# Edges of issue order among the small products of an RWKV-7 and attention block

## The chip, the cores and the metric

The kernel runs on one core of one Trainium2 chip. The metric is device time in microseconds of that core. Before the change the median of three runs is 1573.8 us (1572.52 to 1575.09).

## The reference, cut to what matters

One decoder layer over 1024 tokens of width 1024. An input projection feeds two branches: sliding-window attention, and an RWKV-7 recurrence whose decay and rate come from two low-rank ("lora") products. Both are merged, projected, and followed by a squared-ReLU MLP. The change touches the recurrence alone:

```python
w_log = -softplus(-(decay_bias + tanh(token_shift(w_p, mu_w)) @ decay_up)) - 0.5
decay = exp(-exp(w_log))
a = sigmoid(aaa_bias + token_shift(a_p, mu_a) @ aaa_up)
...
def step(S, inp):                                   # per head, per token
    sa = einsum('bhij,bhj->bhi', S, a_t)
    S = S * w_t + sa[..., None] * b_t + v_t[..., None] * k_t
    return S, einsum('bhij,bhj->bhi', S, r_t)       # y_t
```

The kernel does not step token by token. It cuts the 1024 tokens into 16 chunks of 64, solves each chunk's triangular system by small matrix products, and carries the state from chunk to chunk.

## The kernel before, in words

The program is written in Python with tile pools; a scheduler orders each engine's instructions by priority and by when it reckons that their inputs are ready, and that fixed order is what the chip runs. TensorE (PE) therefore issues in an order chosen at build time.

Up to about 658 us the kernel does projections, attention and the recurrence together. The recurrence is eight *units*: four pairs of heads times two halves of the sequence. Each unit has three steps:

- `unit_e` (L458 on): two lora products with three passes each into two PSUM tiles `ps_l` (L472 to L474); decays, keys and rates from them on ScalarE and VectorE; then chunk scores `ps_s`, two groups (`par` 0 and 1) of eight products, four for each head of the pair, into two PSUM tiles (L519 to L524). Head 0 lies on partitions 0 to 63 and head 1 on 64 to 127, so each product uses 64 rows of the array. Both `ps_l` and `ps_s` come from the PSUM pool tag "s", which has two buffers. VectorE masks the scores into `SA` and `SR`, and solves the 16-wide diagonal blocks row by row in `LT` (L565, L566).
- `unit_m` (L570 on): the 16-wide inverses come back through DRAM as `XT`, are transposed into `XD`, and are widened to 64 by small products `ps_z` and `ps_x`; `ps_g` holds 16 products of the masked scores with the values.
- `unit_c` (L622 on): the *chain* over eight chunks. Per chunk: `ry` (state times keys and receptances), a VectorE add into `G`, two products `pu` (64x64), a VectorE copy into `UV`, product `pd`, two VectorE updates of the state `sbd`, and the next `ry`. Behind it 16 products `py` (128 rows, 64 columns of the array) give the output of the unit (L660 to L665). A `py` needs only the `UV` of its own chunk.

The steps of a unit have high priority. What stands between them on TensorE is filled with low-priority work: projections `ps_m` (128x128 weights, 512 columns), the attention products `ps_t`, `pt_t` and `po`, and transposes `pt`. Nothing in the source binds the products of one `ps_l`, `ps_s` or `py` group to each other: the scheduler is free to take them in any order that their inputs allow.

Of the kernel before, what the change touches and what calls it, by code (L numbers as in the profile page):

```python
# [2 lines left out]

# [55 lines left out]
def hybrid_block(ctx, tc, x_ap, xt_ap, win_ap, lora_ap, wbr_ap, wout_ap, wff1_ap, wff2_ap, cst_ap,  # L59
                 vec_ap, eye_ap, amk_ap, out_ap, dbg=None):  # L60
    nc = tc.nc
    V, A, G, PE = nc.vector, nc.scalar, nc.gpsimd, nc.tensor
# [93 lines left out]
    def mm3(out, pairs):  # L156
        n, last = 0, 3 * len(pairs) - 1
        for (lh, ll), (rh, rl) in pairs:
            for a, b in ((ll, rh), (lh, rl), (lh, rh)):
                PE.matmul(out=out, lhsT=a, rhs=b, start=(n == 0), stop=(n == last))  # L160
                n += 1

    def proj(w, xh, xl, hf, nk=NK):
        ps = pm.tile([P, HALF], F32, tag="m", name="ps_m")
        sl = slice(hf * HALF, (hf + 1) * HALF)
        mm3(ps, [(w[k], (xh[k][:, sl], xl[k][:, sl])) for k in range(nk)])
        return ps
# [71 lines left out]
    def phase1():  # L239
# [27 lines left out]
        g0, g1, full = slice(0, 64), slice(64, 128), slice(0, 128)  # L267
# [190 lines left out]
        def unit_e(p, hf, lw, X):  # L458
            lwh, lwl = lw
            la = ep.tile([P, 2, HALF], F32R, tag="la", name="la")  # L460
# [4 lines left out]
            UV = rp.tile([P, 8, 128], F32, tag="UV", name="UV", bufs=2)  # L465
            BKt = rp.tile([P, 8, 128], F32, tag="BKt", name="BKt", bufs=2)
            SA = rp.tile([P, 2, 8, 64], F32, tag="SA", name="SA", bufs=2)
            SR = rp.tile([P, 2, 8, 64], F32, tag="SR", name="SR", bufs=2)
            bv = rp.tile([P, HALF], F32, tag="bv", name="bv", bufs=2)
            wc = rp.tile([P, 8], F32, tag="wc", name="wc", bufs=2)  # L470
            lps = [pp.tile([P, HALF], F32, tag="s", name="ps_l") for _ in range(2)]
            for n, (a, b) in enumerate(((lwl, 0), (lwh, 1), (lwh, 0))):  # L472
                for ps, rows in zip(lps, (g0, g1)):
                    PE.matmul(out=ps, lhsT=a[rows], rhs=la[rows, b], start=(n == 0), stop=(n == 2))  # L474
            tha = ep.tile([P, HALF], F32, tag="tha", name="tha", bufs=1)
            A.activation(out=tha, in_=lps[1], func=AF.Tanh, scale=0.5, bias=hb[:, 4 + p:5 + p])
            ps = lps[0]
# [39 lines left out]
            ARf = AR.rearrange("p a (b s) c -> p a b (s c)", s=2)  # L517
            BKf = BK.rearrange("p a (b s) c -> p a b (s c)", s=2)
            for par in range(2):  # L519
                pss = [pp.tile([P, 4, 2, 64], F32, tag="s", name="ps_s") for _ in range(2)]  # L520
                for i in range(4):
                    for h in range(2):
                        PE.matmul(out=pss[h][:, i], lhsT=BKf[h * 64:h * 64 + 64, i, par],  # L523
                                  rhs=ARf[h * 64:h * 64 + 64, i, par], start=True, stop=True)  # L524
                for h in range(2):
                    for i, dst in enumerate((SA, SR)):
                        slot = (par + i) % 2
                        V.tensor_mul(out=dst[:, par, h::2, :], in0=pss[h][:, :, slot, :],
                                     in1=mk[:, i].unsqueeze(1).broadcast_to([P, 4, 64]))
# [32 lines left out]
            for t in range(1, 16):  # L562
                n = min(t, 8)
# [58 lines left out]
        def unit_c(p, hf, X):  # L622
            us = slice(hf * HALF, (hf + 1) * HALF)
            ARf, UV, BKt, SR, bv, wc, G0, XT = (X[n] for n in ("ARf", "UV", "BKt", "SR", "bv", "wc", "G0", "XT"))
            Yt = rp.tile([P, 4, 2, 64], F32, tag="Yt", name="Yt", bufs=2)
            for c in range(8):
                par, cp = c % 2, c // 2
                first = hf == 0 and c == 0
                uc, vc = slice(64 * par, 64 * par + 64), slice(64 - 64 * par, 128 - 64 * par)
                cur, nxt = sbd[par], sbd[1 - par]  # L630
                ry = pp.tile([P, 2, 64], F32, tag="r", name="ry", bufs=1)
                Rs = G0[:, cp, :]
                if first:
                    G.memset(Yt[vc, cp], 0.0)
                else:
                    PE.matmul(out=ry.rearrange("p a b -> p (a b)"), lhsT=ARf[:, cp, par], rhs=cur, start=True,  # L636
                              stop=True)
                    V.tensor_add(out=Rs[uc], in0=Rs[uc], in1=ry[uc].rearrange("p a b -> p (a b)"))
                    A.copy(out=Yt[vc, cp], in_=ry[vc])
                pu = pp.tile([P, 128], F32, tag="c", name="pu", bufs=1)  # L640
                for h in range(2):
                    PE.matmul(out=pu[uc, h * 64:h * 64 + 64], lhsT=XT[uc, 2 * cp + h],  # L642
                              rhs=Rs[uc, h * 64:h * 64 + 64], start=True, stop=True)
                V.tensor_copy(out=UV[uc, c, :], in_=pu[uc])
                if hf == 0 or c < 7:
                    pd = pp.tile([P, 128], F32, tag="c", name="pd", bufs=1)
                    PE.matmul(out=pd, lhsT=BKt[:, c], rhs=UV[:, c], start=True, stop=True)  # L647
                    if not first:
                        sw = rp.tile([P, 128], F32, tag="sw", name="sw", bufs=2)
                        A.activation(out=sw, in_=cur, func=AF.Copy, scale=wc[:, c:c + 1])  # L650
                    for h in range(2):
                        hs = slice(h * 64, h * 64 + 64)
                        if first:
                            V.tensor_scalar(out=nxt[hs, hs], in0=pd[hs, hs], scalar1=wc[hs, c:c + 1],
                                            scalar2=None, op0=ALU.mult)
                        else:
                            V.scalar_tensor_tensor(out=nxt[hs, hs], in0=pd[hs, hs], scalar=wc[hs, c:c + 1],
                                                   in1=sw[hs, hs], op0=ALU.mult, op1=ALU.add)
            py = pp.tile([P, 4, 2, 64], F32, tag="y", name="py", bufs=1)
            for cp in range(4):  # L660
                for h in range(2):
                    for par in range(2):
                        vc = slice(64 - 64 * par, 128 - 64 * par)
                        PE.matmul(out=py[vc, cp, h], lhsT=SR[:, par, 2 * cp + h, :],  # L664
                                  rhs=UV[:, 2 * cp + par, h * 64:h * 64 + 64], start=True, stop=True)  # L665
            V.tensor_add(out=Yt, in0=Yt, in1=py)
            if hf == 0:
                dump(f"Yt{p}", Yt)

            Yv = Yt.rearrange("p a b c -> p (a b) c")  # L670
            mean = rp.tile([P, 8], F32, tag="mean", name="mean", bufs=1)
            V.tensor_reduce(out=mean, in_=Yv, axis=AX.X, op=ALU.add)
            V.tensor_scalar(out=mean, in0=mean, scalar1=1.0 / 64, scalar2=None, op0=ALU.mult)
            V.tensor_sub(out=Yv, in0=Yv, in1=mean.unsqueeze(2).broadcast_to([P, 8, 64]))
            ysq = rp.tile([P, 8, 64], F32, tag="ysq", name="ysq", bufs=1)
            A.activation(out=ysq, in_=Yv, func=AF.Square)
            var = rp.tile([P, 8], F32, tag="var", name="var", bufs=1)
            V.tensor_reduce(out=var, in_=ysq, axis=AX.X, op=ALU.add)
            rs = newton(ep, var, 8, 1.0 / 64, GN_EPS, tag="y")
            V.tensor_mul(out=Yv, in0=Yv, in1=rs.unsqueeze(2).broadcast_to([P, 8, 64]))  # L680
            y = rp.tile([P, HALF], F32, tag="ysq", name="y", bufs=1)
            pt = pp.tile([P, 4, 2, 64], F32, tag="y", name="pt", bufs=1)
            for i in range(4):
                PE.transpose(pt[:, i], Yt[:, i], ident)
            for par in range(2):
                A.activation(out=e4(y)[:, :, par, :], in_=pt[:, :, 1 - par, :], func=AF.Identity,
                             scale=v_("lng", p), bias=v_("lnb", p))
            V.tensor_add(out=y, in0=y, in1=bv)
            nc.sync.dma_start(out=yr_d[p][:, us], in_=y)
# [86 lines left out]
    for ct in range(NK):  # L776
        wa = load_w(wbr_ap[ct][:, 0:4], 4)
        wb = load_w(wbr_ap[ct][:, 4:8], 4)
        for hf in range(2):
# [5 lines left out]
            ps = proj(wa, yh, yl, hf, 4)  # L785
            V.scalar_tensor_tensor(out=ga, in0=ga, scalar=1.0, in1=ps, op0=ALU.add, op1=ALU.mult)
            ps = proj(wb, yh[4:], yl[4:], hf, 4)
# [9 lines left out]
    h = [fpool.tile([P, T], F32, name=f"h{k}") for k in range(NK)]  # L797
# [114 lines left out]
    pss = [(pm if t == "m" else pp).tile([P, HALF], F32, tag=t, name="ps_o", bufs=n) for t, n in tags]  # L912
# [43 lines left out]
    for i in range(16):  # L956
# [4 lines left out]
        ps = prod(split_w(a11), "B11")  # L961
# [4 lines left out]
        ps = prod(split_w(s1), "T1")  # L966
# [4 lines left out]
        ps = prod(split_w(s2), "T2")  # L971
# [8 lines left out]
        ps = prod(split_w(s3), "T3")  # L980
# [12 lines left out]
        ps = prod(w4, "B22")  # L993
        V.tensor_add(out=u2, in0=u2, in1=ps)
        c12 = relu_sq("c12", u2, u2, 1)
        ps = prod(split_w(a12), "B21")
        V.tensor_add(out=p1, in0=p1, in1=ps)
        c11 = relu_sq("c11", p1, p1, 0)
        ps = prod(split_w(a22), "T4")
# [3 lines left out]
        for q in range(2):  # L1003
            w = load_w(wff2_ap[i, 2 * q], 4) + load_w(wff2_ap[i, 2 * q + 1], 4)
            for hf in (1, 0):
                sl = slice(hf * HALF, (hf + 1) * HALF)
                for c in range(4):
# [3 lines left out]
                    ps = pp.tile([P, HALF], F32, tag=tag, name="ps_f", bufs=2 if tag == "s" else 1)  # L1011
# [99 lines left out]
```

## Time and profile before

| | us |
|---|---|
| median of three runs | 1573.8 |
| profiled execution, whole time | 1569.57 |
| its span, first to last instruction | 1567.8 |
| TensorE busy | 1538.9 (98%) |
| VectorE busy | 1053.5 (67%) |
| ScalarE busy | 612.2 (39%) |

Busy time is the time in which at least one instruction of the engine is under way. Matmuls overlap, so what one costs is better read in the timeline as the time from its start to the start of what follows it. In that timeline a float32 product appears as two passes (a group of eight scores is "x16"), a float32r product and a transpose as one. The profiled execution is 4.2 us shorter than the median of the runs.

### The profile page before, as it was taken

The page shows a single profiled execution, that of the slowest core. Times are in us where ns is not written, and L with a number is a line of the kernel's source. Part 1 is how long each engine was busy: PE and PEld are TensorE (multiplying, and loading weights), DVE is VectorE, ACT ScalarE, POOL GpSimd, SP SyncE. Part 2 cuts the span into 40 slices and gives each one's busy share as a digit, 9 for nine tenths or more (in the row PEclk, how much of TensorE's full clock was granted, in tenths as well). Part 3 has the DMA queues.
Part 4 walks back from the last instruction along what each step waited for, and adds up shares of the span by engine and source line. Part 5 has one row for each costly group of instructions (what it writes and reads, how often), then busy time and mean ns, then how long its engine had stood idle before and what let it go on. Part 6 is the DMA issues. An engine that isn't in the chain of part 4 may idle for free.

```text
span 1567.8 us, 23163 instructions
## 1 busy us (share of the span) xinstructions
PE 1538.9 (98%) x8588; PEld 1232.9 (79%) x8588; DVE 1053.5 (67%) x2420; ACT 612.2 (39%) x1238; POOL 14.3 (1%) x54
## 2 busy tenths in 40 slices
PE   5999999999999999999999999999999999999999
PEld 5878777777777777788888778888888888888887
DVE  5233877888898775344557587777777777777776
ACT  7333345465545556432224433332333222222222
POOL 1000000000000000000000000000000000000000
PEclk9999999999999999999999999999999999999999
DMA  5465243333221323383442021111111111111113
GB/s 186 155 178 144 95 123 120 103 109 104 82 88 60 97 89 123 109 293 121 143 162 85 20 68 54 43 52 54 54 54 55 43 52 47 54 48 47 47 41 114
DMA packets 108993, 145.72 MB, mean 93 GB/s; under 512 B 27472, under 2 KB 49872, under 8 KB 108880
## 3 DMA queue, kind: packets, MB, share of 16 engines
q1 hardware_dynamic: 108880, 144.23, 28.5%
q8 instruction: 68, 1.11, 0.3%
q14 instruction: 45, 0.37, 0.1%
HBM read 108.54 MB, written 35.65 MB: 92 GB/s over the span
## 4 chain that ended last, share of the span: by engine, by line
PE 93%; DVE 4%; DMA 1%; ACT 1%; issue 0%; SPq 0%; DVEq 0%; ACTq 0%
PE ps_m L160 34%; PE ps_f L160 22%; PE ps_p L160 19%; PE po L160 2%; PE pu L642 2%; PE ps_o L917 1%; PE ps_s L523 1%; PE py L664 1%; PE pk L236 1%; PE pt_t L378 1%; PE ry L636 1%; PE pd L647 1%; PE ps_l L474 1%; PE ps_t L341 1%; PE ps_z L595 1%; PE pt L219 1%
## 5 line engine op out<-in xcount | busy, mean ns | idle before, releaser
L160 PE MATMUL ps_m<-ul,whi 128*128 128x512 f32 x576 | 233.8, 406 | 0.0
L160 PE MATMUL ps_m<-uh,wlo 128*128 128x512 f32 x576 | 233.2, 405 | 0.0
L160 PE MATMUL ps_m<-uh,whi 128*128 128x512 f32 x576 | 232.9, 404 | 0.0
L1013 DVE TENSOR_TENSOR h<-h,ps_f 128x512 f32<-128x512 f32 x256 | 174.5, 687 | 86.3 <-PE ps_f L160 79.8
L145 DVE TENSOR_TENSOR wlo<-wraw,whi 128x512 fp32r<-128x512 f32 x165 | 113.6, 688 | 75.8 <-ACT whi L144 73.6
L144 ACT CAST whi<-wraw 128x512 fp32r<-128x512 f32 x169 | 104.4, 618 | 147.2 <-PE ps_m L160 70.0
L160 PE MATMUL ps_p<-T,whi 128*128 128x512 f32 x512 | 160.3, 394 | 0.0
L160 PEld LDWEIGHTS ps_m<-ul,whi 128*128 128x128 f32 x576 | 108.4, 188 | 20.8 <-issue 0.5
L160 PEld LDWEIGHTS ps_m<-uh,wlo 128*128 128x128 f32 x576 | 108.4, 188 | 20.3 <-issue 0.4
L160 PEld LDWEIGHTS ps_m<-uh,whi 128*128 128x128 f32 x576 | 108.5, 188 | 20.1 <-issue 0.6
L160 PE MATMUL ps_p<-B,whi 128*128 128x512 f32 x384 | 119.6, 392 | 0.0
L160 PEld LDWEIGHTS ps_p<-T,whi 128*128 128x128 f32 x512 | 96.9, 189 | 22.9
L144 ACT CAST whi<-wst 128x512 fp32r<-128x512 f32 x64 | 39.7, 621 | 178.0 <-PE ps_f L160 178.0
L160 PE MATMUL ps_p<-T,wlo 128*128 128x512 f32 x256 | 102.2, 399 | 1.3 <-DVE wlo L145 1.3
L160 PEld LDWEIGHTS ps_p<-B,whi 128*128 128x128 f32 x384 | 72.1, 188 | 16.9
L160 PE MATMUL ps_p<-B,wlo 128*128 128x512 f32 x192 | 76.1, 396 | 0.0
L145 DVE TENSOR_TENSOR wlo<-wst,whi 128x512 fp32r<-128x512 f32 x64 | 44.3, 692 | 39.4 <-ACT whi L144 39.4
L144 ACT CAST whi<-fraw 128x512 fp32r<-128x512 f32 x48 | 29.9, 622 | 87.6 <-PE ps_f L160 61.5
L160 PEld LDWEIGHTS ps_p<-T,wlo 128*128 128x128 f32 x256 | 48.4, 189 | 12.1 <-DVE wlo L145 1.4
L145 DVE TENSOR_TENSOR wlo<-fraw,whi 128x512 fp32r<-128x512 f32 x48 | 33.1, 692 | 31.4 <-ACT whi L144 31.2
L160 PE MATMUL ps_f<-c12h,wlo 128*128 128x512 f32 x128 | 50.4, 394 | 0.0
L160 PE MATMUL ps_f<-c22h,wlo 128*128 128x512 f32 x128 | 50.4, 394 | 0.0
(305 smaller groups left out, 3190.9 us busy)
## 6 DMA issues: line engine op xcount, KB each, us to landing
wraw<-win SPq DMA_DIRECT2D x72, 256.0 KB, 3.0
fraw<-wff SPq DMA_DIRECT2D x64, 256.0 KB, 2.8
wraw<-wff SPq DMA_DIRECT2D x64, 256.0 KB, 2.6
gate_d<-gt SPq DMA_DIRECT2D x32, 256.0 KB, 2.1
z_d<-zt SPq DMA_DIRECT2D x24, 256.0 KB, 2.3
xt<-x SPq DMA_DIRECT2D x8, 512.0 KB, 5.5
la<-wa_d SPq DMA_DIRECT2D x8, 512.0 KB, 4.6
aq<-q_d SPq DMA_DIRECT2D x8, 512.0 KB, 4.3
```

The lines of the kernel that those rows point to most:

```text
L144: A.copy(out=hi, in_=raw)
L145: (eng or V).tensor_sub(out=lo, in0=raw, in1=hi.bitcast(F32))
L160: PE.matmul(out=out, lhsT=a, rhs=b, start=(n == 0), stop=(n == last))
L219: PE.transpose(pt[:, i * 128:(i + 1) * 128], xs[i][:, k * 128:(k + 1) * 128], ident)
L236: PE.matmul(out=ps_out[:, col + 2 * i:col + 2 * i + 2], lhsT=sq[:, i * 128:(i + 1) * 128], rhs=c_("ind"), start=True, stop=True)
L341: PE.matmul(out=ps[:, i, w0:], lhsT=q_[:, g, j], rhs=k_[:, 2 + g, w0:], start=True, stop=False)
L378: PE.transpose(pt[:, sb, i], sm[:, i, sb * 128:(sb + 1) * 128], ident)
L474: PE.matmul(out=ps, lhsT=a[rows], rhs=la[rows, b], start=(n == 0), stop=(n == 2))
L523: PE.matmul(out=pss[h][:, i], lhsT=BKf[h * 64:h * 64 + 64, i, par], rhs=ARf[h * 64:h * 64 + 64, i, par], start=True, stop=True)
L595: PE.matmul(out=ps[uc, l], lhsT=SA[uc, par, l], rhs=XD[uc, l], start=True, stop=True)
L642: PE.matmul(out=pu[uc, h * 64:h * 64 + 64], lhsT=XT[uc, 2 * cp + h], rhs=Rs[uc, h * 64:h * 64 + 64], start=True, stop=True)
L1013: V.tensor_add(out=h[ct][:, sl], in0=h[ct][:, sl], in1=ps)
```

## The change

A helper `in_order` issues a list of matmuls with an edge from each to the next one: it binds their order on TensorE, adds no semaphore, and leaves other instructions free to stand between them. It is used for

- the six `ps_l` products of a unit: half a (rows 0 to 63, decay) and half b (rows 64 to 127, rate) in turn,
- the eight `ps_s` products of a group: head 0 and head 1 in turn,
- the two `pu` products of a chunk,
- the 16 `py` products of a unit, which also get an edge from the last `pu` of the chain, so that none of them stands inside the chain.

```diff
+    def in_order(mms, after=None):
+        for out, lhsT, rhs, start, stop in mms:
+            with tc.issue_after(after) if after is not None else nullcontext():
+                after = PE.matmul(out=out, lhsT=lhsT, rhs=rhs, start=start, stop=stop).ins
+        return after
...
-            for n, (a, b) in enumerate(((lwl, 0), (lwh, 1), (lwh, 0))):
-                for ps, rows in zip(lps, (g0, g1)):
-                    PE.matmul(out=ps, lhsT=a[rows], rhs=la[rows, b], start=(n == 0), stop=(n == 2))
+            in_order([(ps, a[rows], la[rows, b], n == 0, n == 2)
+                      for n, (a, b) in enumerate(((lwl, 0), (lwh, 1), (lwh, 0)))
+                      for ps, rows in zip(lps, (g0, g1))])
...
-                for i in range(4):
-                    for h in range(2):
-                        PE.matmul(out=pss[h][:, i], lhsT=BKf[h * 64:h * 64 + 64, i, par],
-                                  rhs=ARf[h * 64:h * 64 + 64, i, par], start=True, stop=True)
+                in_order([(pss[h][:, i], BKf[h * 64:h * 64 + 64, i, par], ARf[h * 64:h * 64 + 64, i, par], True, True)
+                          for i in range(4) for h in range(2)])
...
-                for h in range(2):
-                    PE.matmul(out=pu[uc, h * 64:h * 64 + 64], lhsT=XT[uc, 2 * cp + h],
-                              rhs=Rs[uc, h * 64:h * 64 + 64], start=True, stop=True)
+                last = in_order([(pu[uc, h * 64:h * 64 + 64], XT[uc, 2 * cp + h], Rs[uc, h * 64:h * 64 + 64], True,
+                                  True) for h in range(2)])
...
-            for cp in range(4):
-                for h in range(2):
-                    for par in range(2):
-                        vc = slice(64 - 64 * par, 128 - 64 * par)
-                        PE.matmul(out=py[vc, cp, h], lhsT=SR[:, par, 2 * cp + h, :],
-                                  rhs=UV[:, 2 * cp + par, h * 64:h * 64 + 64], start=True, stop=True)
+            outs = [slice(64, 128), slice(0, 64)]
+            in_order([(py[outs[par], cp, h], SR[:, par, 2 * cp + h, :],
+                       UV[:, 2 * cp + par, h * 64:h * 64 + 64], True, True)
+                      for cp in range(4) for h in range(2) for par in range(2)], last)
```

Every engine keeps the same instructions; only their order differs, on TensorE between the instructions that run at 147 and at 658 us before. In the changed kernel the bound matmuls all stand under line 166, and other lines are 3 to 6 higher.

TensorE, one chunk of the chain of the fourth unit, before: from its `pd` to the `pu` of the next chunk.

```order
L647 MATMUL pd<-UV,BKt 128x128
L664 MATMUL py<-UV,SR 64x64
L160 MATMUL ps_m<-uh_144,wlo 128x512
L160 MATMUL ps_m<-ul_152,whi 128x512
L160 MATMUL ps_m<-uh_144,whi 128x512
L160 MATMUL ps_m<-uh_145,wlo 128x512
L160 MATMUL ps_m<-ul_153,whi 128x512
L636 MATMUL ry<-sbd_489,AR 128x128
L160 MATMUL ps_m<-uh_145,whi 128x512
L160 MATMUL ps_m<-uh_146,wlo 128x512
L160 MATMUL ps_m<-ul_154,whi 128x512
L642 MATMUL pu<-G_3681,XT 64x64 x2
```

One `py`, whose `UV` has just come, stands between `pd` and the work that fills the time until `ry`.

The same engine and unit after the change: from the last `pd` of the chain on.

```order
L650 MATMUL pd<-UV,BKt 128x128
L160 MATMUL ps_m<-uh_149,wlo 128x512
L160 MATMUL ps_m<-ul_157,whi 128x512
L160 MATMUL ps_m<-uh_149,whi 128x512
L160 MATMUL ps_m<-uh_142,wlo 128x512
L160 MATMUL ps_m<-ul_150,whi 128x512
L640 MATMUL ry<-sbd_489,AR 128x128
L160 MATMUL ps_m<-uh_142,whi 128x512
L160 MATMUL ps_m<-uh_143,wlo 128x512
L160 MATMUL ps_m<-ul_151,whi 128x512
L166 MATMUL pu<-G_3681,XT 64x64 x2
L166 MATMUL py<-UV,SR 64x64 x13
```

The `py` is gone from between `pd` and `ry`, and 13 of the unit's 16 stand behind its last `pu`; one `ps_m`, the other three and the 16 `ps_g` of the next unit follow.

In the whole program before, the 128 `py` stand in 65 runs: 33 of one, 31 of three and one of two, 57 of them right behind a `pd`. After, they stand in 14 runs, all behind the last `pu` of a unit: two of 16, and six groups of 16 that are cut once. Adjacent matmuls of different tile shape become fewer by 98 (424 before, 326 after), while entries from a 128x128 product into one of 64 rows and 128 columns rise from 27 to 35.

TensorE, the second score group of the second unit, before; `ps_s_1886` is head 0, `ps_s_1887` head 1.

```order
L523 MATMUL ps_s_1886<-AR_1795,BK_1796 128x128 x4
L160 MATMUL ps_m_1765<-uh2_144,whi_1727 128x512
L523 MATMUL ps_s_1887<-AR_1795,BK_1796 128x128 x4
L160 MATMUL ps_m_1765<-uh3_145,wlo_1728 128x512
L549 MATMUL pt_1913<-cst_80,BK_1796 128x128 x4
```

The two heads run one after the other, four products each.

The same group after.

```order
L166 MATMUL ps_s_1886<-AR_1795,BK_1796 128x128
L160 MATMUL ps_m_2143<-uh0_142,whi_2133 128x512
L160 MATMUL ps_m_2143<-uh1_143,wlo_2134 128x512
L166 MATMUL ps_s_1887<-AR_1795,BK_1796 128x128
L166 MATMUL ps_s_1886<-AR_1795,BK_1796 128x128
L166 MATMUL ps_s_1887<-AR_1795,BK_1796 128x128
L166 MATMUL ps_s_1886<-AR_1795,BK_1796 128x128
L166 MATMUL ps_s_1887<-AR_1795,BK_1796 128x128
L166 MATMUL ps_s_1886<-AR_1795,BK_1796 128x128
L166 MATMUL ps_s_1887<-AR_1795,BK_1796 128x128
```

The first product still goes ahead alone, since the second PSUM buffer comes free later; the other seven now alternate. Of the 16 score groups seven alternated without a gap before and five do after. Nine groups ran in blocks of one head or in pieces before, and 11 are cut after, seven of these in the form above. Of the eight lora groups one alternates without a gap after; in seven half a's first product goes ahead alone (up to 61 other matmuls before half b's), and the other five follow alternately, in four units with one more gap.

## Rows read from the trace of the kernel before

**Rows 1.** Page, chain that ended last: share of the span by engine.
```profile
PE 93%; DVE 4%; DMA 1%; ACT 1%; issue 0%; SPq 0%; DVEq 0%; ACTq 0%
```

**Rows 2.** Windows: length, busy PE, PEld, DVE, ACT, POOL, clock, DMA; changed stretch.
```profile
147.00:658.00 511.00, 505.50 (x4018) 387.24 (x4018) 389.78 (x1357) 274.21 (x671) 6.64 (x34) 1.00 0.32 100
```

**Rows 3.** Waits of PE, 147 to 658 us: total, times, longest.
```profile
PE ps_s L523 <- DVE SR L528: 1.2, 2, 0.7
...
PE ry L636 <- DVE sbd L657: 0.2, 1, 0.2
```

**Rows 4.** Timeline of PE, one chunk: start, duration, engine, line, operation.
```profile
393.30 0.38 PE L647 MATMUL pd<-UV,BKt 128*128 128x128 f32 x2
393.62 0.33 PE L664 MATMUL py<-UV,SR 128*64 128x64 f32 x2
393.87 0.50 PE L160 MATMUL ps_m<-uh,wlo 128*128 128x512 f32 x1
394.21 0.39 PE L160 MATMUL ps_m<-ul,whi 128*128 128x512 f32 x1
...
395.14 0.38 PE L636 MATMUL ry<-sbd,AR 128*128 128x128 f32 x2
...
395.59 0.40 PE L160 MATMUL ps_m<-uh,wlo 128*128 128x512 f32 x1
```

**Rows 5.** Timeline of PE, a run of three py behind pd.
```profile
336.43 0.38 PE L647 MATMUL pd<-UV,BKt 128*128 128x128 f32 x2
336.74 0.45 PE L664 MATMUL py<-UV,SR 128*64 128x64 f32 x6
337.12 0.51 PE L160 MATMUL ps_m<-uh,wlo 128*128 128x512 f32 x1
337.46 0.40 PE L160 MATMUL ps_m<-ul,whi 128*128 128x512 f32 x1
```

**Rows 6.** Timeline of PE, 16 products ps_g in one run.
```profile
291.01 1.15 PE L579 MATMUL ps_g<-UV,SA 64*64 64x64 f32 x32
292.09 0.51 PE L160 MATMUL ps_m<-uh,wlo 128*128 128x512 f32 x1
```

**Rows 7.** Timeline of PE: scores alternating, four of one head, one alone.
```profile
409.78 1.16 PE L523 MATMUL ps_s<-AR,BK 64*128 64x128 f32 x16
410.87 0.51 PE L160 MATMUL ps_m<-uh,wlo 128*128 128x512 f32 x1
...
193.39 1.13 PE L523 MATMUL ps_s<-AR,BK 64*128 64x128 f32 x8 [0.56 <-DVE SR L528]
194.44 0.49 PE L160 MATMUL ps_m<-uh,whi 128*128 128x512 f32 x1
...
275.79 0.49 PE L523 MATMUL ps_s<-AR,BK 64*128 64x128 f32 x2
276.20 0.33 PE L664 MATMUL py<-UV,SR 128*64 128x64 f32 x2
```

**Rows 8.** Timeline of PE: lora, three of one half, then four alternating.
```profile
147.14 0.49 PE L474 MATMUL ps_l<-la,lwl 64*128 64x512 f32 x1
...
148.03 0.83 PE L236 MATMUL pk<-cst,sq 128*128 128x2 f32 x6
...
475.14 0.49 PE L474 MATMUL ps_l<-la,lwl 64*128 64x512 f32 x1
...
475.81 0.49 PE L636 MATMUL ry<-sbd,AR 128*128 128x128 f32 x2
```

**Rows 9.** Timeline of DVE, the state update in the chunk of rows 4.
```profile
393.79 0.58 DVE L657 SCALAR_TENSOR_TENSOR sbd<-pd,wc,sw 64x64 f32<-64x64 f32 x2 [0.24 <-PE pd L647]
```

**Rows 10.** Timeline of DVE, then PE: the inverse of one unit arrives.
```profile
510.25 0.71 DVE L591 STREAM_TRANSPOSE XD<-XT 128x512 f32<-128x512 f32 x1
...
511.18 1.15 PE L595 MATMUL ps_z<-XD,SA 64*64 64x64 f32 x32
```

More of the change, by code (lines that the diff above doesn't have):

```diff
@@ L1 @@
-from contextlib import ExitStack
+from contextlib import ExitStack, nullcontext
 import math
```

## The prediction

> **What bounds the kernel now.** I read the chain of waits first, then the windows, then TensorE's waits, and the timeline last. The chain that ended last is 93% TensorE and 4% VectorE [rows 1]. The change moves matmuls only between 147 and 658 us, so the question is what bounds that stretch. In its 511 us TensorE is busy 505.5 and VectorE 389.8, and the clock is at its full level, 1.00, which is 2.4 GHz [rows 2]. TensorE's waits there are small: the scores waited 1.2 us in all for a buffer, the chain once, for 0.2 us [rows 3]. So the stretch costs what the matmuls cost in the order in which they stand. No instruction is removed or added; the whole effect must come from what each costs beside its neighbours, less the waits that a tighter order opens. The reader should therefore look in the timeline at start-to-start times, and not at the durations, which overlap.
>
> **The y products.** In the chunk of rows 4 the time from `pd` to the second matmul behind its `py` is 394.21 - 393.30 = 0.91 us. A float32 product of the same shape without a `py` stands a little later: from `ry` to the second `ps_m` behind it is 395.59 - 395.14 = 0.45 us [rows 4]. One `py` thus costs 0.46 us there, of which 0.25 us lies between its own start and the next matmul's; the rest is that `pd` and the next `ps_m` run longer. A run of three costs 337.46 - 336.43 = 1.03, less the same 0.45, that is 0.58 us, and 0.38 us of it by its own start-to-start [rows 5]. The order before has 19 runs of one and 12 of three between a `pd` and a `ps_m`: 19 x 0.46 + 12 x 0.58 = 15.7 us. The other 14 of one, 19 of three and one of two stand beside other things (attention products, transposes, other small products), where part of the price is due anyway; I take their own time, 14 x 0.25 + 19 x 0.38 + 0.3 = 11.0 us. Together 26.7 us. After the change there are eight groups of 16. The nearest row is `ps_g`: 16 small products in 292.09 - 291.01 = 1.08 us [rows 6]; it has 64 rows where `py` has 128, but the same 64 columns and 64 outputs, and alternates places in the same way. That gives 8 x 1.08 = 8.6 us. Six groups are cut once; a cut is one more way out of and into the small shape, and between nothing and 0.46 us I take 0.3, so 1.8 us. Saved: 26.7 - 10.4 = 16.3 us. The lower bound has all 65 runs at their own time (20.3 us) against 10.4: 9.9 us. The upper has all at full price (33.5 us) and the cuts free: 24.9 us.
>
> In rows 4 a change of tile shape and back costs about 0.4 us beyond what a product in a run costs (1.08/16 = 0.07). The Trainium skill, TensorEngine Tiling (Array Packing), section Tiling Modes, states this as a rule: a change of mode, not just of tile, drains TensorE. By that rule the 98 changes fewer are the gain, at half of 0.4 us each some 20 us, near my sum; it also speaks against the part on scores below, where such entries rise from 27 to 35.
>
> **The chunk scores.** A group that alternates costs 410.87 - 409.78 = 1.09 us; four products of one head cost 194.44 - 193.39 = 1.05, so a group in two blocks 2.1; one product alone costs 276.20 - 275.79 = 0.41 us [rows 7]. Before: seven groups at 1.09 and nine at about 2.0 (some of the nine alternate in part): 25.6 us. After: five at 1.09; seven with one product ahead, 0.41 + 1.05 = 1.46; four in other pieces, which I put at 1.7: 5.5 + 10.2 + 6.8 = 22.5 us. Eight more entries at 0.1 to 0.2 us take back about 1. I take a gain of 2 us. Bounds: if all 16 cost 1.09, a gain of 8; if the 11 cut ones cost 2.1, a loss of 3, or 5 with the entries.
>
> **The lora products.** Three of one half cost 148.03 - 147.14 = 0.89 us, so a group in blocks 1.78; four in turn cost 475.81 - 475.14 = 0.67, so six 1.0 us [rows 8]; one alone I take from the scores, 0.41 [rows 7]. Before: four groups in blocks and four alternating in part, which I put at 1.5: 13.1 us. After: seven with one ahead and five in turn, 0.41 + 1.0, one at 1.0, and 0.2 for each of four gaps: 11.7 us. Gain 1.4 us, between 0 and 5. Half a's result, which the decays need, now comes after half b has its buffer; in the longest case 61 other matmuls stand between. I cost this at nothing, because the scores that need it stand many matmuls later; where that cover is gone it is a wait at `ps_s`. The `pu` pairs already stand together: nothing.
>
> The sum is 16.3 + 2 + 1.4 = 19.7 us of TensorE time, with 5 and 38 as the ends of all bounds together.
>
> **What comes back as waits.** Two covers become thinner. First, each chunk: `ry` needs `sbd`. In rows 4 and 9 the update ends at 393.79 + 0.58 = 394.37 and `ry` starts at 395.14, 0.77 us later. Without the `py`, 0.46 us of this goes and 0.31 is left (0.19 where three stood). There are 60 such places, and one waited before [rows 3]; behind a waiting `ry` the whole queue of TensorE stands. VectorE runs other work between, so some updates will be late by a few tenths. Between nothing and 60 x 0.2 = 12 us I take 3. Second, each unit: `XD` ends at 510.25 + 0.71 = 510.96 and `ps_z` starts at 511.18 [rows 10], so this unit's products come hardly later than their input. If the way of the inverse through VectorE and DRAM does not move, TensorE gives back there what it won in the unit, 19.7 / 8 = 2.5 us, in all eight 19.7. But VectorE is busy only 389.8 of 511 us [rows 2] and itself waits for `pd` in part [rows 9], so most of its work moves forward with TensorE; I take 2. Together 5 us come back.
>
> The `py` at the end of a unit make its output later by at most one group, 1.1 us. The norm and the store that follow are hidden by projections that fill TensorE; without them it would cost that 1.1 us at the last unit alone. No DMA is added.
>
> Net 19.7 - 5 = 14.7 us. The profiled execution took 1569.6 us (its span 1567.8 and 1.8 around it), so I expect 1554.9 of such an execution; the median of the runs is 4.2 higher, so 1573.8 - 14.7 = 1559.1 us.
>
> **The rivals.**
> - *More comes back.* The tighter order meets late inputs at most chunks and half the units: 8 + 5 = 13 us come back, 1567 us. For it: covers of 0.3 us in rows 4 and 9, and 0.2 in rows 10. Against: VectorE has 24% free.
> - *All comes back.* The period of a unit is set by the inverse and not by TensorE; then the 19.7 us turn into waits at `ps_z` and `ry`: 1574 us. Against it: TensorE waits for almost nothing now [rows 3], while a chain that set the period would already show in them.
> - *Slower: the strict turns stall the queue.* With alternation the second product of a group must wait until its own PSUM buffer is free, and TensorE issues in order, so everything behind it waits too. Before, a whole head could run in that time; now one product does, 0.41 us. There are 24 such groups; from 19.7 / 24 = 0.8 us of wait each the gain is gone, and at 1.0 us each the kernel takes 1573.8 + 24 - 19.7 = 1578 us. For it: two such waits exist, up to 0.7 us [rows 3]. Against: the order after puts two or more `ps_m` between the first product and the second in most groups.
> - *More than my sum.* Each change of tile shape costs the full half of 0.46 us wherever it stands: 98 x 0.23 = 22.5, with the 3.4 us of scores and lora 25.9, and nothing comes back: 1548 us. It is what the rule of the Trainium skill on changes of mode (TensorEngine Tiling (Array Packing), section Tiling Modes) would do here; rows 4 to 6 bear it out so far.
>
> **How the numbers follow.** My forecast has 62% (its own range 1552 to 1565), more coming back 16%, all coming back 10%, the stall 5%, more than the sum 7%. The range from 1550 to 1568 holds the first two and part of the last, and leaves out what is above. About 0.2% (3 us) is what a measurement of this kernel can tell from no change. Faster by more than that: forecast, more coming back and more than the sum, with a little taken for ends: 85%; within it 9%; slower 6%.
>
> **What the profile after would show.** Right: `py` in eight groups of about 1.1 us, its busy time by line far under the present one; TensorE busy in the changed stretch about 485 us; `pd` followed by `ps_m` at 0.45 to 0.55 us for both; waits of TensorE for `sbd`, `XD` or `SR` of some 5 us. Wrong: groups of `py` near 3 us each, or a TensorE whose idle time before `ry`, `ps_z` and `ps_s` grows by more than 10 us.

## The result and the profile after

The changed kernel takes 1558.3 us (median of four, 1557.45 to 1559.07), the kernel before in the same comparison 1574.2 us (1572.52 to 1575.09): a ratio of 0.990, with a 95% interval of 0.988 to 0.992. It is faster by 16 us; 1559.1 was forecast, in a range of 1550 to 1568. The profiled execution took 1557.75 us (span 1556.0); that is only 11.8 us under the profiled one of before, which was 4.2 us faster than the median of its kernel. What the traces account for below is therefore the 11.8, and not the whole 16.

The chain that ended last, as in [rows 1]:

```profile
PE 89%; DVE 7%; DMA 2%; ACT 1%; issue 1%; SPq 0%; DVEq 0%; ACTq 0%
```

TensorE still sets the time, but VectorE's share has grown from 4 to 7%, as it would if some inputs now came late. The windows, with the columns of [rows 2]; the changed stretch now ends near 646 us:

```profile
147.00:646.00 499.00, 490.10 (x4022) 370.47 (x4022) 386.16 (x1358) 274.60 (x673) 6.71 (x34) 1.00 0.34 105
```

The stretch is 12 us shorter at the same clock (13.2 us between the same two instructions). What lies ahead of it is the same 147 us. What lies behind it takes 910.0 us instead of 909.8, or 1.3 more from the second of those two instructions on. TensorE's idle time in it rises from 511.0 - 505.5 = 5.5 to 8.9 us. Its waits there, as in [rows 3] (total, times, longest):

```profile
PE ps_t L347 <- DMA ak<-k_d: 1.8, 2, 1.5
PE ps_s L166 <- DVE SR L532: 0.9, 2, 0.6
PE pt L553 <- DVE SR L532: 0.8, 2, 0.5
PE ps_z L615 <- DVE DZ L611: 0.7, 1, 0.7
PE ry L640 <- DVE sbd L660: 0.7, 3, 0.3
```

The scores wait no longer than before, and `ry` three times instead of once. By this view hardly anything has come back. It misleads, as the weight loads show further down.

The y products: TensorE's timeline at the end of a unit, `pu` being the last step of its chain. One group in one piece, one cut:

```profile
285.60 0.44 PE L166 MATMUL pu<-G,XT 64*64 64x64 f32 x4
285.97 1.15 PE L166 MATMUL py<-UV,SR 128*64 128x64 f32 x32
287.05 1.15 PE L583 MATMUL ps_g<-UV,SA 64*64 64x64 f32 x32
...
395.91 0.44 PE L166 MATMUL pu<-G,XT 64*64 64x64 f32 x4
396.28 1.03 PE L166 MATMUL py<-UV,SR 128*64 128x64 f32 x26
397.24 0.50 PE L160 MATMUL ps_m<-uh,whi 128*128 128x512 f32 x1
397.67 0.45 PE L166 MATMUL py<-UV,SR 128*64 128x64 f32 x6
398.05 1.15 PE L583 MATMUL ps_g<-UV,SA 64*64 64x64 f32 x32
```

Sixteen `py` take 287.05 - 285.97 = 1.08 us, what [rows 6] show for `ps_g`. The cut group takes 0.96 + 0.38, so the cut costs 0.26 in the time of the `py`, and the `ps_m` inside it takes 0.43 where one in a row of `ps_m` takes 0.23: some 0.46 together. (Four of the six groups are cut by a `pd` instead, which then takes 0.42 instead of 0.13; their `py` lose 0.15: some 0.44 together.)

A chunk from which the `py` has gone, for [rows 4], and its state update on VectorE, for [rows 9]:

```profile
393.52 0.38 PE L650 MATMUL pd<-UV,BKt 128*128 128x128 f32 x2
393.65 0.48 PE L160 MATMUL ps_m<-uh,wlo 128*128 128x512 f32 x1
393.97 0.40 PE L160 MATMUL ps_m<-ul,whi 128*128 128x512 f32 x1
...
394.90 0.38 PE L640 MATMUL ry<-sbd,AR 128*128 128x128 f32 x2
395.03 0.48 PE L160 MATMUL ps_m<-uh,whi 128*128 128x512 f32 x1
...
393.94 0.58 DVE L660 SCALAR_TENSOR_TENSOR sbd<-pd,wc,sw 64x64 f32<-64x64 f32 x2
```

`pd` to the second `ps_m` is 0.45 us, as forecast, where [rows 4] have 0.91. The update ends at 394.52 and `ry` starts 0.38 us later, where 0.77 lay between. One chunk earlier in the same unit even that is gone; here TensorE, then VectorE:

```profile
389.33 0.44 PE L650 MATMUL pd<-UV,BKt 128*128 128x128 f32 x2
...
390.67 0.40 PE L160 MATMUL ps_m<-ul,whi 128*128 128x512 f32 x1
391.01 0.46 PE L640 MATMUL ry<-sbd,AR 128*128 128x128 f32 x2
391.22 0.48 PE L160 MATMUL ps_m<-uh,whi 128*128 128x512 f32 x1
...
389.62 0.75 DVE L512 SCALAR_TENSOR_TENSOR kkn<-k,nkk,pt 128x512 f32<-128x512 f32 x1
390.29 0.57 DVE L660 SCALAR_TENSOR_TENSOR sbd<-pd,wc,sw 64x64 f32<-64x64 f32 x2
```

The update stood behind `kkn`, ended at 390.86, and `ry` starts 0.15 us later. Of the 60 `ry`, 38 start 0.12 to 0.16 us behind their update (five more 0.05 us); before, two did (and one 0.05 us). This is how an update that came last looks, so `ry` waited. The `ps_m` ahead of it takes 0.34 us from start to start instead of 0.23, and `ry` itself 0.21 instead of 0.13. Yet the profile shows no idle time here, since the recorded 0.40 us of that `ps_m` reach past the start of `ry`. The wait shows on the weight load of `ry`, whose weights `sbd` is. That group by line, of before and then of after (busy us, mean ns | idle before, and what ended it):

```profile
L636 PEld LDWEIGHTS ry<-sbd,AR 128*128 128x128 f32 x120 | 21.0, 188 | 6.1 <-issue 1.0 <-DVE sbd L657 0.7 <-DVE r L412 0.4
```

```profile
L640 PEld LDWEIGHTS ry<-sbd,AR 128*128 128x128 f32 x120 | 18.7, 188 | 13.2 <-issue 4.8 <-DVE sbd L660 2.2 <-ACT ph L386 1.0
```

The loads of `ry` stand idle for 7.1 us more than before. Start-to-start times on TensorE give less. Of the 41 chunks in which a `ps_m` stands ahead of `ry`, 32 start `ry` within 0.2 us of its update (two of 39 before); the 41 `ps_m` take 12.4 us instead of 41 x 0.233 = 9.6. The 60 `ry` take 14.9 instead of 11.0, but one of them holds a wait of another kind, for an input of `ps_t` that a DMA brings:

```profile
425.47 0.39 PE L640 MATMUL ry<-sbd,AR 128*128 128x128 f32 x2
427.40 0.36 PE L347 MATMUL ps_t<-ak,aq 128*128 128x256 f32 x1 [1.53 <-DMA ak<-k_d]
```

Without it the `ry` take 13.4. Together 2.8 + 2.4 = 5.2 us; the 19 chunks with another product ahead of `ry` are counted here only by their `ry`. (The second trace of the change, after_again, has 13.2 us of idle time before the loads and 13.6 us of `ry` with 0.2 us of that wait.)

Why the updates come last is to be read from the same chunks. Of all 60, 47 start `ry` within 0.2 us of the update (five before). In 32 of the 47 VectorE begins the update 0.42 to 0.55 us behind the start of its `pd`, which was the usual time before as well (half of the 60 within 0.49). So in these VectorE is on time: the way from `pd` over the two updates (0.58 us) to `ry` takes some 1.2 us, and less work than that now stands in between (from `pd` to `ry` half of the chunks took 1.56 us or more before and 1.27 after). In the other 15 the update begins later than usual, as in the chunk shown behind `kkn`.

Scores, for [rows 7]: one product ahead, then the other seven in turn (each is counted as x2).

```profile
197.53 0.46 PE L166 MATMUL ps_s<-AR,BK 64*128 64x128 f32 x2 [0.29 <-DVE SR L532]
197.92 0.50 PE L160 MATMUL ps_m<-uh,whi 128*128 128x512 f32 x1
198.26 0.40 PE L160 MATMUL ps_m<-uh,wlo 128*128 128x512 f32 x1
198.59 1.16 PE L166 MATMUL ps_s<-AR,BK 64*128 64x128 f32 x14
199.67 0.50 PE L160 MATMUL ps_m<-ul,whi 128*128 128x512 f32 x1
```

That is 0.39 + 1.08 = 1.47 us (forecast 1.46). The inverse, for [rows 10], on VectorE and then TensorE:

```profile
507.04 0.71 DVE L595 STREAM_TRANSPOSE XD<-XT 128x512 f32<-128x512 f32 x1
...
508.12 1.15 PE L599 MATMUL ps_z<-XD,SA 64*64 64x64 f32 x32
```

Between its end and `ps_z` lie 0.37 us, where 0.22 lay: the inverse moved forward with TensorE.

The balance of the stretch, in sums of start-to-start times on TensorE before and after:

| products | before, us | after, us | difference |
|---|---|---|---|
| `py` | 20.4 | 9.9 | -10.5 |
| `pd` | 19.2 | 11.2 | -8.0 |
| `ps_s` | 25.6 | 23.1 | -2.5 |
| `ps_l` (lora, gate) | 19.8 | 18.3 | -1.5 |
| `ry` | 11.0 | 14.9 | +3.9 |
| `ps_m` | 262.3 | 265.7 | +3.5 |
| `po` | 25.2 | 26.8 | +1.6 |

These sum to -13.5 us, against the 13.2 by which the stretch is shorter. The waits for `ps_t`'s input fall into `ps_m` before (2.6 us) and into `ry` after (1.5). Without them `ry` is 2.4 us longer and `ps_m` some 6; 2.8 of these 6 stand ahead of `ry`, and what the rest waits for is not shown one by one.

### The profile page after: what moved, and what is told of

Its sections match the earlier page's. It is cut to its first block, busy times and chain, and to the rows that moved or that the text cites. A ratio compares the mean times of both kernels' runs of the same rounds, so it can differ in the third digit from the quotient of the medians.

```text
span 1556.0 us, 23162 instructions
## 1 busy us (share of the span) xinstructions
PE 1523.9 (98%) x8588; PEld 1216.3 (78%) x8588; DVE 1049.1 (67%) x2420; ACT 611.6 (39%) x1238; POOL 14.4 (1%) x54
## 3 DMA queue, kind: packets, MB, share of 16 engines
q1 hardware_dynamic: 108880, 144.23, 28.7%
## 4 chain that ended last, share of the span: by engine, by line
PE 89%; DVE 7%; DMA 2%; ACT 1%; issue 1%; SPq 0%; DVEq 0%; ACTq 0%
PE ps_m L160 31%; PE ps_f L160 23%; PE ps_p L160 20%; PE pu L166 1%; PE ps_o L918 1%; PE po L160 1%; PE ry L640 1%; DMA ak<-k_d 1%; PE pt_t L384 1%; PE pk L242 1%; PE pd L650 1%; PE ps_s L166 1%; DVE LT L569 1%; PE ps_l L166 1%; PE ps_x L604 1%
```

## The experiments

Each kernel is the changed one with the edit shown, and ratios are to the kernel before. The 95% interval of a ratio is some 0.0012 to 0.002 to each side (2 to 3 us), so smaller differences between variants are not told apart.

**e1_y_only**: the y and `pu` products keep the new order, scores and lora products the old loops.

```
-in_order([(ps, a[rows], la[rows, b], ...) ...])      # lora; scores likewise
+for n, (a, b) in enumerate(((lwl, 0), (lwh, 1), (lwh, 0))):
+    for ps, rows in zip(lps, (g0, g1)):
+        PE.matmul(out=ps, lhsT=a[rows], rhs=la[rows, b], ...)
```

> Only the y products (and the pu pairs) are bound; scores and lora products are free as before. Theory A (the gain is what matmuls cost beside their neighbours, and most of it is y): 16.3 us of y saved, 4 come back in the chunks, so about 1562 us, 12 under before; py in the stretch about 10 us start-to-start instead of 20.4, pd about 11 instead of 19.2. Rival B (scores and lora in turn carry the gain): 1570 or more.

Measured: 1561.94 us against 1572.17, ratio 0.9928 (0.9916 to 0.9941), a gain of 10.2 us (11 by the ratio). `py` takes 9.9 and `pd` 10.8 us, as in the whole change. `ry` takes 12.9 and the idle time before its loads rises to 11.9 us; 43 of the 60 `ry` start within 0.2 us of their update. The time comes back already with this part alone.

**e2_pairs_only**: the reverse; `py` and `pu` are free, scores and lora in order.

```
-in_order([(py[outs[par], cp, h], ...) ...], last)    # pu likewise
+for cp in range(4):
+    for h in range(2):
+        for par in range(2):
+            PE.matmul(out=py[vc, cp, h], ...)
```

> Only scores and lora products are bound in turn; y and pu are free as before, so py stands inside the chain (64 runs). Theory A: scores 2 and lora 1.4 us less, little comes back: 1571 us, 3 under before. Rival B: 1562 or less. Rival C (the strict turns stall the queue): not below before, with waits at ps_s or ps_l.

Measured: 1566.26, ratio 0.9961 (0.9949 to 0.9973), a gain of 5.9 us, twice the forecast. `ps_s` loses 2.9 us and `ps_l` 2.5; `ry` stays at 10.7, and its loads at 5.0 us of idle time (6.1 before). 10.2 + 5.9 = 16.1 us is near the whole change's 15.9: within the 2 to 3 us to which each is known, the two parts add up. They also part the causes: only where the `py` leave the chunks does `ry` come too early for its update (here 4 of the 60 start within 0.2 us of it).

**e4_y_blocks**: the same 16 `py` together, but all eight of one column half and then all eight of the other.

```
-for cp in range(4) for h in range(2) for par in range(2)], last)
+for par in range(2) for cp in range(4) for h in range(2)], last)
```

> As the change, but the 16 y products stand by place: all eight of par 0 (columns 64 to 127), then all eight of par 1. Theory A1 (what counts is that they stand together, away from 128x128 products): as the change, 1558 us. Theory A2 (within a run the alternation of places counts too, since the next product's weights can only be loaded beside a running product of another place): a product in a block costs like pu behind pu, 0.165 us and more instead of 0.06, so 128 x 0.1 = 13 us more: about 1571 us.

Measured: 1560.92, ratio 0.9928 (0.9916 to 0.9940), about 4 us above the whole change by the ratios. TensorE at the unit whose `py` stand in one piece above:

```profile
289.95 0.44 PE L166 MATMUL pu<-G,XT 64*64 64x64 f32 x4
290.32 1.90 PE L166 MATMUL py<-UV,SR 128*64 128x64 f32 x32
292.15 0.86 PE L583 MATMUL ps_g<-UV,SA 64*64 64x64 f32 x22
```

The group takes 1.83 us instead of 1.08, all `py` 15.5 instead of 9.9. So standing together saves the larger part, and taking turns between the column halves is worth 5.6 us of `py` more: a `py` costs 0.117 us behind one of the same half and 0.058 behind one of the other.

**e6_y_after_pd**: the `py` are bound behind the unit's last `pd` instead of its last `pu`.

```
-PE.matmul(out=pd, lhsT=BKt[:, c], rhs=UV[:, c], start=True, stop=True)
+last = PE.matmul(out=pd, lhsT=BKt[:, c], rhs=UV[:, c], start=True, stop=True).ins
```

> As the change, but the y products of a unit are bound behind the last pd of the chain instead of the last pu, so that pd no longer cuts the group (5 runs of 16 instead of 2). Theory: each cut costs 0.3 us, three cuts fewer, 1 us less: 1557 us. Rival: pd of the last chunk waits for UV with nothing in front of it, and the 0.6 us of that wait stands bare in four units: 1560 us.

Measured: 1557.51, ratio 0.9905 (0.9892 to 0.9918); not told apart from the change. `py` takes 9.4 us. Where exactly the group stands behind the chain makes no difference that these runs tell apart.

**e3_no_lora**: the lora products keep the old loops (as in e1), the rest is new.

> As the change, but the lora products are free as before. Theory (lora in turn is worth 2 to 2.5 us): 0.9915 of before, lora products in the stretch 20 us start-to-start again instead of 18.3. Rival (half a's result, held back by half b's buffer, costs what the turns win): as the change, 0.990.

Measured: 1556.82, ratio 0.9888 (0.9872 to 0.9904): no loss, against 1.5 us of gain that the lora turns should have brought. `ps_l` does take 21.5 us instead of 18.3, but `ps_m` 263.7 instead of 265.7 and `ps_s` 21.9 instead of 23.1 (`ry` 13.1, against 13.4 without the wait behind it). The scheduler put the queue together differently, and the time came back in products that the edit does not name; which of the differences did it is not shown.

**e7_bank_s, e7_again**: one score group in two takes its second PSUM buffer from the tag of `py`, which has one and is free until the chain ends, so that its second product need not wait.

```
-pss = [pp.tile([P, 4, 2, 64], F32, tag="s", name="ps_s") for _ in range(2)]
+tags = (("s", 2), ("y", 1) if par else ("s", 2))
+pss = [pp.tile([P, 4, 2, 64], F32, tag=t, name="ps_s", bufs=n) for t, n in tags]
```

> As the change, but the second tile of the second score group takes the PSUM bank of y (free of y products until the chain ends) instead of the shared tag, so that the first product has not to go ahead alone: 10 of 16 score groups alternate without a gap, against five. Theory (a product alone and the way out and in cost 0.3 to 0.6 us a group): five groups at 0.4 less, 2 us less than the change, 0.9885 of before. Rival (the bank is held by the norm of the unit before, and the scores come later): no gain or 1 to 3 us more, with waits at ps_s.

Measured: 1553.91, ratio 0.9869 (0.9850 to 0.9887). The group of rows 197.53 above now runs in one piece:

```profile
196.72 1.16 PE L166 MATMUL ps_s<-AR,BK 64*128 64x128 f32 x16 [0.70 <-DVE SR L533]
197.81 0.66 PE L554 MATMUL pt<-cst,BK 128*128 128x128 f32 x4
```

1.09 us instead of 1.47, though its first product waits 0.70 us instead of 0.29; nine of the 16 groups do so in the trace (five in the changed kernel), and `ps_s` takes 21.2 instead of 23.1 us. Run once more:

> The kernel with the y bank for the second score group once more, on another chip: if its lead over the change (0.987 against 0.990) is its own, 0.986 to 0.988 of before; if it was that chip, 0.989 to 0.991.

Measured: 1553.61, ratio 0.9886 (0.9866 to 0.9906). By the ratios the two lie some 5 and 2 us under the change, and the intervals overlap with its own. The traces point the same way: between the same two instructions the stretch takes 492.2 and 492.3 us in the two here, 497.6 and 496.4 in the two of the change (after_again below is the second). A lead is likely and not settled.

**e8_wlo_pool**: in this phase the low halves of the weights are subtracted on GpSimd and not on VectorE, to take work away from in front of the state updates.

```
-(eng or V).tensor_sub(out=lo, in0=raw, in1=hi.bitcast(F32))
+(eng or weng[0]).tensor_sub(out=lo, in0=raw, in1=hi.bitcast(F32))   # weng[0] = G in phase1()
```

> As the change, but the low parts of the weights (wlo) are computed on GpSimd instead of VectorE between 147 and 646 us, some 29 us less for VectorE. Theory L (what came back in the chunks is the fixed way from pd through two updates to ry): ry in the stretch stays near 15 us start-to-start, the time as the change within 2 us. Theory Q (it is VectorE's other work ahead of the update): ry falls to 12 or less and the time by 3 to 6 us. If GpSimd is late with wlo, TensorE waits for wlo and it gets slower.

Measured: 1571.55, ratio 0.9990 (0.9979 to 1.0001): the whole gain is lost. The subtraction by line, and the window (columns as above):

```profile
L147 POOL TENSOR_TENSOR wlo<-wraw,whi 128x512 fp32r<-128x512 f32 x41 | 54.7, 1333 | 286.0 <-ACT whi L146 226.7 <-PE ry L642 22.5 <-DMA ak<-k_d 15.5
```

```profile
147.00:646.00 499.00, 481.06 (x3969) 362.68 (x3968) 380.97 (x1315) 273.44 (x667) 60.89 (x75) 0.99 0.33 101
```

and the subtraction in the changed kernel:

```profile
L145 DVE TENSOR_TENSOR wlo<-wraw,whi 128x512 fp32r<-128x512 f32 x42 | 28.7, 685 | 8.6 <-ACT whi L144 8.4
```

VectorE was to lose 28.7 us of work; it is busy only 5.2 us less, since its other operations became longer. So this run does not do what it was meant to. `ry` stays at 13.1 us (13.4 in the change without the wait behind it), while TensorE's idle time doubles, from 8.9 to 17.9 us, with new waits for VectorE (`pu` for `G`, 3.0 us; `ps_s` for `SR`, 2.9; `pt` for `rnx`, 2.7). This run thus cannot tell whether work queued on VectorE makes the updates late. The count of chunks above does: in 32 of 47 it does not.

**after_again, e9_bank_no_lora, e10_bank_after_pd, e11_bank_no_lora_pd**: the change once more, and e7's edit together with e3's, with e6's, and with both.

> The changed kernel itself once more, beside the three below on the same chip: 0.990 of before, as the first time.

> The y bank for the second score group, and lora products free as before. If the two are independent: 0.987 (the bank) and 0.000 to 0.001 less for the lora products, 0.986 to 0.987 of before. If the lora turns do help: 0.988 to 0.989.

> The y bank for the second score group, and the y products behind the last pd. If the two are independent: 0.5 to 1 us less than the bank alone, 0.9865 of before.

> All three: the y bank for the second score group, lora products free, y products behind the last pd (eight runs of 16). Fewest changes of tile shape of all (315). If the parts add: 0.985 to 0.987 of before, about 1551 us. If the chunks' waits set the time by now: 0.988 as the bank alone or above.

Measured against 1572.78: 1557.82 (0.9906, 0.9889 to 0.9923), 1558.17 (0.9902, 0.9887 to 0.9917), 1555.14 (0.9887, 0.9872 to 0.9902) and 1555.57 (0.9891, 0.9876 to 0.9905). Edits that looked good singly do not add: e9 loses what e7 seemed to win, and e11, with the fewest changes of tile shape of all (315, against 327 in the changed kernel), is not the fastest. Each edit also makes the scheduler put the rest of the queue together anew; that this is what separates the variants by 1 to 4 us is likely, but no run isolates it.

## Why the prediction was right

The forecast was 14.7 us and the runs show 16. The mechanism was the one named. Two terms were mis-sized in opposite directions, so that the total came out this near is in part luck; and the sums below are of profiled executions 11.8 us apart, so some 4 us of the 16 stand in no trace.

- *Bound.* Right: the gain lies in the stretch, in TensorE's order, at an unchanged clock.
- *y products, 16.3 us.* The price behind `pd` was right (0.45 us is left, as said), as was 1.08 us a group; a cut cost about 0.45, near the upper end and not the 0.3 taken. The term came out at 10.5 + 8.0 = 18.5 us: I charged the 34 runs of `py` beside other small work with their own time only. But 26 of them stand behind a `pd` and lengthen it too, and `pd` alone lost 8.0 us. The e1 run shows the same two sums without the other parts.
- *Scores 2, lora 1.4 us.* 2.5 and 1.5 us by the sums, so right in size. Alone, in e2, the two bring 2.9 and 2.5, and its time falls by 5.9 us. Together with the `py`, e3 cannot show a gain of the lora turns at all: a term this small is lost among the other differences of order.
- *Back at the chunks, 3 us.* Mis-sized: about 5 us by the starts (5.2), 7 by the loads' idle time (7.1). The step at fault is the cover. I took 0.77 us from the one chunk of rows 4 and 9 and left 0.31 of it. But of the 60 chunks of before only seven have a longer cover; half have 0.44 us or less, and 47 have less than 0.61, which is the 0.46 of a `py` and the 0.15 that is left where `ry` waits. After the change 47 come within 0.2 us of their update. I also argued from VectorE's free quarter. In 32 of these 47 VectorE is on time, so its free share has little to do with it; what counts is the way from `pd` to `ry` against the work that is left to stand in between.
- *Back at the units, 2 us.* The inverse moved with TensorE, and the waits at `ps_z` come to 1.0 us (0.7 shown above, 0.3 for another input). Against 0.2 before, that is under 1 us.
- *What no term covers.* By the balance 22.5 us were won and 13.2 are left, so some 9 came back where 5 were taken. Besides the chunks' 5, `ps_m` and `po` grew elsewhere by some 5 us, and a shorter wait for `ps_t`'s input gave 1 back.
- *The signs.* TensorE busy about 485 us was wrong (490.1 of 499): hidden waits count as busy, and I had taken coming back as idle time. The listed waits for `sbd` and `SR` come to 2.4 us and not to some 5.

Of the rivals, *more comes back* has its mechanism at the chunks and not its time, since the y term was larger. *All comes back* fell: TensorE still sets the time. *Strict turns stall* fell: `ps_s` waits 0.9 us for `SR`, 1.2 before, and e2, where the turns stand alone, gains. *More than my sum* had each change of tile shape at one price. Against it: by the traces e2 has five changes more than the kernel before (430 against 425; the count ahead of the prediction gives 424 and 326 for the two kernels, one less each) and is 5.9 us faster; e1 has one fewer than the change (326 against 327) and e4 three more (330), and both are some 4 us slower. The Trainium skill, TensorEngine Tiling (Array Packing), section Tiling Modes, says that a change of mode drains TensorE; the 0.46 us that went with the `py` of rows 4 agree with it. But that count alone gives no time here: which place of the array a product takes after its neighbour matters too (0.117 against 0.058 us in e4).

## What to carry to other kernels

Where an in-order engine is full and nothing waits, look for small products scattered between large ones, and price them by start-to-start times, their neighbours' too: gathered in one group that alternates between places of the array, they cost about a third of that here (9.9 us for `py`, where 20.4 and 8.0 more on `pd` went). Before counting the gain, look at which inputs arrived under the products you take away: at every place, not at one, and not by an engine's free share. Part of the gain will return there (5 to 7 of some 22 us here). Differences of a few us between reorderings that leave a scheduler free need repeats before an edit is credited with them.

## What was not expected of the hardware

- A wait of TensorE shorter than the tail of the matmul ahead shows neither as idle time nor among the waits: 0.7 us of `ry` waits are listed where start-to-start times lose 5.2. The idle time of the weight loads (from 6.1 to 13.2 us) shows it.
- Eight `py` in the same column half take 0.117 us each and 16 alternating 0.068, the first and last among them; between them it is 0.058.
- A 128x512 subtraction takes GpSimd 1333 ns and VectorE 685, and while GpSimd does 41 of them VectorE's products of `LT` take 309 ns on average instead of 269 (by the profile, in which spans on GpSimd are rough). The Trainium skill, SBUF — State Buffer, section Who interferes with whom, has a VectorE operation with two inputs in SBUF contend with a GpSimd one that reads SBUF, the later one blocked at a port that they share; VectorE's 24 us of added time beside 54.7 us of these subtractions go with that, though no run here tells a lock from slower sharing.
